# Two-layer streaming encoder in float32: the tail of the layer norms and the sums of the first one

## The chip, the cores and the metric

The kernel runs on one core of one Trainium2 chip. The metric is device microseconds of one execution. The kernel before takes 2613.07 us, the median of three runs (2607.23 to 2613.16). A core has a matrix engine (TensorE, PE in the profile, with its weight loads as PEld), a vector engine (VectorE, DVE), an engine for functions of one input (ScalarE, ACT), a general engine (GpSimd, POOL) and an engine that here issues most of the transfers (SyncE, SP). Each runs its own list of instructions in order, and they wait for one another by semaphores. Products accumulate in PSUM; everything else lies in SBUF.

## The reference, cut to what matters

One sequence of 1024 frames with 1024 channels passes through an RWKV-7 mixer, an MLP, a diagonal state-space mixer (S5) with a gated output, and a second MLP. After each of the four stands a layer norm of the residual sum:

```python
def layer_norm(x, g, b):
    xf = x.astype(jnp.float32)
    mu = jnp.mean(xf, axis=-1, keepdims=True)
    var = jnp.mean(jnp.square(xf - mu), axis=-1, keepdims=True)
    return ((xf - mu) * lax.rsqrt(var + LN_EPS) * g + b).astype(x.dtype)

x = layer_norm(DN_ALPHA * x + rwkv7_time_mix(x, ...), g0, b0)
x = layer_norm(DN_ALPHA * x + sq_relu_mlp(x, w1, w2), g1, b1)
x = layer_norm(DN_ALPHA * x + s5_mix(x, ...), g2, b2)
x = layer_norm(DN_ALPHA * x + sq_relu_mlp(x, w1, w2), g3, b3)
```

The last four lines are condensed; everything is float32.

## The kernel before, in words

Channels lie on the 128 partitions, frames along the free dimension. The 1024 frames are two halves of 512, called A and B below; a half of the activations is eight tiles of 128 channels by 512 frames (hA, hB).

A dense product is made of three TensorE products (L199). A weight tile `wraw` is loaded by SyncE, ScalarE rounds it to `whi` (L153) and VectorE makes the rest `wlo` = wraw − whi (L154). The input is split the same way into operand tiles (oAh and oAl for half A, oBh and oBl for B, qbuf in the MLPs). TensorE then adds hi·hi, hi·lo and lo·hi. There are two buffers for wraw and three each for whi and wlo, so a weight's next load waits for the split of an earlier one.

The recurrence of the first mixer is done in chunks, for each of which VectorE and ScalarE make the tables (KB, AR, PL, ldsg, elementwise work), TensorE makes matrices from them (pA), and a chain of small products steps the state: pR, pX, pU, pO (L716 to L737), each released by a copy `vsa` on ScalarE or VectorE. Half A's frames come first. After the fifth of its eight blocks the output product of half A and its layer norm are placed, and then half A's first MLP may begin while the recurrence of half B goes on.

Layer norm is called seven times by `layer_norm`, and the last half's last norm is a function of its own. The calls, in order of time: first norm, half A (at about 700 us) and half B (about 1180); second norm, A and B; third norm, A (about 1840) and B (about 1935); fourth norm, A. The first and the third make the operand tiles of the MLP behind them (`split_out`), the second and the fourth do not. A norm's steps are:

- mean: the eight tiles are added to one by GpSimd (two adds) and VectorE (five); a product with a matrix of ones, `pm`, sums over channels and spreads the mean over all partitions; VectorE subtracts it from the eight tiles (L883).
- variance: ScalarE squares each tile, VectorE and GpSimd add the squares to one tile (L891, L892), and four products of one column each, `pq` (L895), sum over channels with the frames on the partitions. VectorE adds epsilon (rs, L897), GpSimd takes the power −1/2, ScalarE spreads it (rb), and TensorE turns it into `pr`, the factor of each frame on all partitions.
- tail: VectorE multiplies each tile by pr (L906), ScalarE applies gain and offset in place (L907), and if operands are wanted `operand` splits the result: ScalarE rounds to the high part (L153), VectorE makes the low part (L154), except for tiles 1, 3 and 5 (`LNG`), whose low part GpSimd makes.

pm, pq and pr take turns in one PSUM bank (tag "l"). The squares have two buffers of each of two tags.

The order of each engine's instructions is not the order of the code. A scheduler places them by a rank: the code runs under `rank(...)`, lower numbers first, and a model of the engines' times decides among what is ready. The first norm, half A, has rank −1 (`LN1R`), ahead of all; the MLPs and the other norms come by their own ranks. The order is fixed when the kernel is built.

Of the kernel before, what the change touches and what calls it, by code (L numbers as in the profile page):

```python
# [8 lines left out]
F32 = mybir.dt.float32  # L9
F32R = mybir.dt.float32r  # L10
AF = mybir.ActivationFunctionType
# [8 lines left out]
KT = 8  # L20
# [7 lines left out]
LN1R = -1  # L28
WO0R = 99000
S5R = 300000  # L30
LNG = (1, 3, 5)
LNT = (2, 5)
TB = 2
JB = 4
# [39 lines left out]
def trunk(ctx, tc, A):  # L74
# [39 lines left out]
    def vec(n, k):  # L114
        i = PV.index(n)
        return pv[:, i, k : k + 1]
# [111 lines left out]
    def optile(H, hl):  # L228
        if H == 1:
            return sp.tile([128, HT], F32R, tag="oB" + hl, name="oB" + hl, bufs=8)  # L230
        return ap.tile([128, HT], F32R, tag="oA" + hl, name="oA" + hl, bufs=8)

    def operand(src, H=0, e=None):
        h, l = optile(H, "h"), optile(H, "l")
        split(src, h, l, e)
        return h, l
# [566 lines left out]
    def core():  # L803

        pg = rwkv_proj(0)
        next(pg)
        bulk.clear()
        with rank(3000):
            cur = elem(0)
        with rank(5000):  # L810
            amat(cur)
            invert(cur)
        with rank(100000):
            run(pg)
        last = None
        for m in range(8):
            if m == PB:
                with rank(100000):
                    run(rwkv_proj(1))
            if m == W0B:  # L820

                with rank(WO0R):
                    first_out.append(wo(0))
                with rank(LN1R):
                    first_out.append(layer_norm(first_out[0], 0, 0))
            base = m * 10000
            with rank(base + RK[0]):
                kbtrans(cur)
            nxt = None
            if m < 7:  # L830
                with rank(base + RK[1]):
                    nxt = elem(m + 1)
            if last and m in GB:
                with rank(base + RK[2]):
                    gnorm(last, 1)
            with rank(base):
                chain(cur, 0)
            if last and m not in GB:
                with rank(base + RK[2]):
                    gnorm(last, 1)  # L840
            if nxt and m < 6:
                with rank(base + RK[3]):
                    amat(nxt)
            with rank(base + RK[4]):
                chain(cur, 1)
            with rank(base + RK[5]):
                gnorm(cur, 0)
            if nxt:
                with rank(base + RK[6]):
                    if m == 6:  # L850
                        amat(nxt)
                    invert(nxt)
            last, cur = cur, nxt
        with rank(base + 8000):
            gnorm(last, 1)
# [4 lines left out]
            return ap.tile([128, HT + 1], F32, tag="xs", name="hA", bufs=8)[:, 0:HT]  # L860
        return sp.tile([128, HT], F32, tag="hB", name="hB", bufs=8)

    def layer_norm(h, gi, H, split_out=True):
        g, b = f"g{gi}", f"b{gi}"

        def lt(name, tag="la"):
            return tp.tile([128, HT], F32, tag=tag, name=name, bufs=2)

        def plt(name):
            return pl.tile([128, HT], F32, tag="l", name=name)  # L870

        a, b2 = lt("sa"), lt("sb")
        G.tensor_add(a, h[0], h[1])
        G.tensor_add(a, a, h[2])
        V.tensor_add(b2, h[3], h[4])
        for t in h[5:7]:
            V.tensor_add(b2, b2, t)
        V.tensor_add(b2, b2, h[7])
        V.tensor_add(a, a, b2)
        pm = plt("pm")  # L880
        PE.matmul(pm, ones_c, a, start=True, stop=True)
        for t in h:
            V.tensor_sub(t, t, pm)  # L883
        sa = [lt("sq0"), lt("sq1")]
        for k, t in enumerate(h):
            if k < 2:
                S.activation(sa[k], t, AF.Square)
            else:
                q = lt("sq", "m")
                S.activation(q, t, AF.Square)  # L890
                (G if k % 2 else V).tensor_add(sa[k % 2], sa[k % 2], q)  # L891
        V.tensor_add(sa[0], sa[0], sa[1])  # L892
        pq = plt("pq")
        for t in range(4):
            PE.matmul(pq[:, t : t + 1], sa[0][:, t * 128 : (t + 1) * 128], ones_c[:, 0:1], start=True, stop=True)  # L895
        rs = tp.tile([128, 4], F32, tag="rs", name="rs")
        V.tensor_scalar(rs, pq[:, 0:4], LN_EPS, None, op0=ALU.add)  # L897
        G.tensor_tensor(rs, rs, mhalf[:, 0:4], op=ALU.pow)
        rb = lt("rb").rearrange("p (t n) -> p t n", t=4)
        S.copy(rb, rs.unsqueeze(2).broadcast_to([128, 4, 128]))  # L900
        pr = plt("pr")
        for t in range(4):
            PE.transpose(pr[:, t * 128 : (t + 1) * 128], rb[:, t], ident)
        ops = []
        for k, t in enumerate(h):
            V.tensor_mul(t, t, pr)  # L906
            S.activation(t, t, AF.Identity, bias=vec(b, k), scale=vec(g, k))  # L907
            if split_out:
                ops.append(operand(t, H, G if k in LNG else V))
        return ops  # L910

    def last_norm(h, gi, c):
# [688 lines left out]
```

## Time and profile before

| | |
|---|---|
| median of three runs | 2613.07 us (2607.23 to 2613.16) |
| the profiled execution | 2617.01 us |
| its span in the trace | 2615.3 us |
| its mean granted TensorE clock | 0.971 |
| TensorE busy | 95% |
| VectorE, ScalarE, GpSimd busy | 69%, 47%, 17% |

In a row of the windows stand the start and end of a stretch, its length, then busy time and number of instructions of PE, PEld, DVE, ACT and POOL, the granted clock, the share of the DMA engines and the gigabytes per second. A row of the timeline has the start, the busy time of the instructions that it joins (their number behind x), the engine, the line, what is written and read, the shape, and in brackets the engine's idle time just before and what ended it. A row that begins with a line number sums up all instructions of a kind: number, shortest, median and longest duration in nanoseconds, first and last start.

### The profile page before, as it was taken

The page shows a single profiled execution, that of the slowest core. Times are in us where ns is not written, and L with a number is a line of the kernel's source. Part 1 is how long each engine was busy: PE and PEld are TensorE (multiplying, and loading weights), DVE is VectorE, ACT ScalarE, POOL GpSimd, SP SyncE. Part 2 cuts the span into 40 slices and gives each one's busy share as a digit, 9 for nine tenths or more (in the row PEclk, how much of TensorE's full clock was granted, in tenths as well). Part 3 has the DMA queues.
Part 4 walks back from the last instruction along what each step waited for, and adds up shares of the span by engine and source line. Part 5 has one row for each costly group of instructions (what it writes and reads, how often), then busy time and mean ns, then how long its engine had stood idle before and what let it go on. Part 6 is the DMA issues. An engine that isn't in the chain of part 4 may idle for free.

```text
span 2615.3 us, 43837 instructions
## 1 busy us (share of the span) xinstructions
PE 2473.6 (95%) x16624; PEld 2005.4 (77%) x16624; DVE 1813.5 (69%) x3459; ACT 1216.5 (47%) x2171; POOL 443.5 (17%) x372
## 2 busy tenths in 40 slices
PE   7999989999889999999999999999999999999997
PEld 5778767788667888776787888887777888888876
DVE  7366766787986766989886555777587555555576
ACT  7554575654454443345534333433464333433344
POOL 3121432332322001001000000201212111111011
PEclk9998979999989999999999999999999999999998
DMA  4765545554322324445465333253222111111133
GB/s 146 254 219 152 166 162 188 188 190 157 100 74 84 95 85 137 131 129 157 133 227 190 97 97 97 89 190 133 86 88 78 54 47 52 55 51 53 49 96 114
DMA packets 206291, 319.69 MB, mean 122 GB/s; under 512 B 20096, under 2 KB 80640, under 8 KB 206080
## 3 DMA queue, kind: packets, MB, share of 16 engines
q1 hardware_dynamic: 204928, 314.79, 38.2%
q8 instruction: 131, 2.15, 0.3%
q10 hardware_dynamic: 1152, 2.10, 0.2%
q14 instruction: 80, 0.66, 0.1%
HBM read 252.85 MB, written 63.96 MB: 121 GB/s over the span
## 4 chain that ended last, share of the span: by engine, by line
PE 61%; DVE 11%; DMA 3%; issue 2%; ACT 2%; POOL 1%; SPq 0%; ACTq 0%; DVEq 0%; POOLq 0%
PE d L199 46%; PE d L1048 9%; DVE wlo L154 2%; DMA wraw<-in_mw_dram 1%; DVE hA L1011 1%; DMA tt<-tT 1%; PE pA L608 0%; ACT whi L153 0%; PE py L1384 0%; PE pbu L1332 0%; PE pu L1320 0%; PE pk L1281 0%; DVE o L780 0%; DVE sq L891 0%; DVE xh L654 0%
## 5 line engine op out<-in xcount | busy, mean ns | idle before, releaser
L153 ACT CAST whi<-wraw 128x512 fp32r<-128x512 f32 x524 | 324.4, 620 | 680.3 <-PE d L199 465.0
L154 DVE TENSOR_TENSOR wlo<-wraw,whi 128x512 fp32r<-128x512 f32 x524 | 381.3, 728 | 260.2 <-ACT whi L153 255.2
L199 PE MATMUL d<-qbuf,whi 128*128 128x512 f32 (+1 forms) x1344 | 410.3, 389 | 12.8 <-DVE hA L1011 7.8
L199 PE MATMUL d<-oAh,whi 128*128 128x512 f32 (+1 forms) x768 | 308.9, 409 | 16.8 <-ACT ev L429 7.5
L199 PE MATMUL d<-oAh,wlo 128*128 128x512 f32 (+1 forms) x768 | 308.6, 406 | 10.2 <-DVE wlo L154 7.2
L199 PE MATMUL d<-oAl,whi 128*128 128x512 f32 (+1 forms) x768 | 308.0, 404 | 1.4 <-DVE oAl L154 1.4
L199 PEld LDWEIGHTS d<-qbuf,whi 128*128 128x128 f32 x1344 | 245.6, 190 | 67.6 <-DVE hA L1011 11.0
L199 PE MATMUL d<-qbuf,wlo 128*128 128x512 f32 (+1 forms) x672 | 257.2, 385 | 1.3 <-DVE wlo L154 1.1
L199 PE MATMUL d<-oBh,wlo 128*128 128x512 f32 x512 | 203.9, 399 | 3.4 <-DVE wlo L154 3.4
L199 PE MATMUL d<-oBh,whi 128*128 128x512 f32 x512 | 203.1, 397 | 2.4 <-ACT whi L153 2.0
L199 PE MATMUL d<-oBl,whi 128*128 128x512 f32 x512 | 201.4, 393 | 0.0
L199 PEld LDWEIGHTS d<-oAh,whi 128*128 128x128 f32 (+1 forms) x768 | 147.1, 193 | 53.9 <-ACT ev L429 9.7
L199 PEld LDWEIGHTS d<-oAh,wlo 128*128 128x128 f32 (+1 forms) x768 | 146.9, 192 | 46.0 <-DVE wlo L154 10.5
L199 PEld LDWEIGHTS d<-oAl,whi 128*128 128x128 f32 (+1 forms) x768 | 147.4, 193 | 33.3 <-DVE oAl L154 3.0
L199 PE MATMUL d<-qh,wlo 128*128 128x512 f32 x384 | 151.5, 395 | 0.0
L199 PE MATMUL d<-ql,whi 128*128 128x512 f32 x384 | 150.7, 392 | 0.0
L199 PE MATMUL d<-qh,whi 128*128 128x512 f32 x384 | 149.4, 389 | 0.0
L199 PEld LDWEIGHTS d<-qbuf,wlo 128*128 128x128 f32 x672 | 127.2, 190 | 27.9 <-DVE wlo L154 3.2
L1011 DVE TENSOR_TENSOR hB<-hB,d 128x512 f32<-128x512 f32 (+1 forms) x168 | 105.0, 633 | 33.2 <-PE d L199 31.4
L199 PEld LDWEIGHTS d<-oBh,wlo 128*128 128x128 f32 x512 | 96.8, 189 | 27.9 <-DVE wlo L154 4.8
L199 PEld LDWEIGHTS d<-oBh,whi 128*128 128x128 f32 x512 | 97.0, 189 | 24.0 <-ACT whi L153 2.6
L1011 DVE TENSOR_TENSOR hA<-hA,d 128x512 f32<-128x512 f32 x144 | 97.5, 682 | 24.2 <-PE d L199 23.1
(476 smaller groups left out, 5079.2 us busy)
## 6 DMA issues: line engine op xcount, KB each, us to landing
wraw<-in_mw_dram SPq DMA_DIRECT2D x376, 256.0 KB, 2.7
wraw<-in_glu_dram SPq DMA_DIRECT2D x64, 256.0 KB, 2.7
low<-wlo SPq DMA_DIRECT2D x52, 256.0 KB, 2.8
wlo<-low SPq DMA_DIRECT2D x52, 256.0 KB, 3.6
raw<-in_mw_dram SPq DMA_DIRECT2D x48, 256.0 KB, 2.6
wraw<-in_wk_dram SPq DMA_DIRECT2D x32, 256.0 KB, 3.8
wraw<-in_wr_dram SPq DMA_DIRECT2D x32, 256.0 KB, 3.6
wraw<-in_wv_dram SPq DMA_DIRECT2D x32, 256.0 KB, 4.5
```

The costliest lines, as they stand in the source:

```text
L153: S.copy(hi, src)
L154: (e or V).tensor_sub(lo, src, hi.bitcast(F32))
L199: bulk.append((PE.matmul(p, w, x, **kw).ins, x.shape[-1]))
L1011: V.tensor_add(z, z, p)
L1048: PE.matmul(p, w[:, k], x, start=not add and k + j == 0, stop=k == 3 and j == 2, skip_group_check=True)
```

## The change

All seven norms get another tail. VectorE multiplies deviation, gain and the frame's factor in one three-input operation. Where operands are wanted, ScalarE adds the offset and writes the rounded high part straight into the operand tile, and VectorE makes the low part, (t + b) − hi, in one three-input operation, for all eight tiles; GpSimd makes none. After that ScalarE adds the offset in place for the residual, tile by tile.

The first norm of half A alone (`by_pe`) also gets other sums. The mean's product takes three tiles in turn (the sum of tiles 0 to 2, the sum of 3 to 6, and tile 7) instead of their sum. The squares are not added by VectorE and GpSimd: each of the eight squared tiles goes through four products of one column that accumulate in pq, 32 instead of four.

```diff
-LNG = (1, 3, 5)
...
-                    first_out.append(layer_norm(first_out[0], 0, 0))
+                    first_out.append(layer_norm(first_out[0], 0, 0, True, True))
...
-    def layer_norm(h, gi, H, split_out=True):
+    def layer_norm(h, gi, H, split_out=True, by_pe=False):
...
-        V.tensor_add(b2, b2, h[7])
-        V.tensor_add(a, a, b2)
+        if by_pe:
+            parts = [a, b2, h[7]]
+        else:
+            V.tensor_add(b2, b2, h[7])
+            V.tensor_add(a, a, b2)
+            parts = [a]
         pm = plt("pm")
-        PE.matmul(pm, ones_c, a, start=True, stop=True)
+        for k, t in enumerate(parts):
+            PE.matmul(pm, ones_c, t, start=k == 0, stop=k == len(parts) - 1)
         for t in h:
             V.tensor_sub(t, t, pm)
...
+        pq = plt("pq")
+        if by_pe:
+            for k, t in enumerate(h):
+                q = lt("sq", ("la", "m")[k % 2])
                 S.activation(q, t, AF.Square)
-                (G if k % 2 else V).tensor_add(sa[k % 2], sa[k % 2], q)
-        V.tensor_add(sa[0], sa[0], sa[1])
...
+                for t4 in range(4):
+                    PE.matmul(pq[:, t4 : t4 + 1], q[:, t4 * 128 : (t4 + 1) * 128], ones_c[:, 0:1],
+                              start=k + t4 == 0, stop=k == KT - 1, skip_group_check=True)
+        else:
...
+                    (G if k % 2 else V).tensor_add(sa[k % 2], sa[k % 2], q)
+            V.tensor_add(sa[0], sa[0], sa[1])
...
         for k, t in enumerate(h):
-            V.tensor_mul(t, t, pr)
-            S.activation(t, t, AF.Identity, bias=vec(b, k), scale=vec(g, k))
+            V.scalar_tensor_tensor(t, t, vec(g, k), pr, op0=ALU.mult, op1=ALU.mult)
             if split_out:
-                ops.append(operand(t, H, G if k in LNG else V))
+                hi, lo = optile(H, "h"), optile(H, "l")
+                S.activation(hi, t, AF.Identity, bias=vec(b, k))
+                V.scalar_tensor_tensor(lo, t, vec(b, k), hi.bitcast(F32), op0=ALU.add, op1=ALU.subtract)
+                ops.append((hi, lo))
+        for k, t in enumerate(h):
+            S.activation(t, t, AF.Identity, bias=vec(b, k))
         return ops
```

The order of the instructions moves with it. Line numbers after the change are one less up to the norm and 16 more behind it. TensorE around the first norm, before (from the recurrence's pX to the norm's pq):

```order
L721 MATMUL pX<-o,XT 64x64 x8
L555 MATMUL pn<-ident,sq 128x128 x4
L726 MATMUL pU<-vsa,kbt 64x64 x8
L735 MATMUL pO<-st,AR 64x64 x8
L737 MATMUL pO<-vsa,AT_7145 64x64 x8
L584 MATMUL pb<-rksel,kf 64x1
L608 MATMUL pA<-AR,KB 128x128
L584 MATMUL pb<-rksel,kf 64x1 x15
L716 MATMUL pR<-vsa,AT_7145 64x64 x8
L608 MATMUL pA<-AR,KB 128x128 x7
L721 MATMUL pX<-o,XT 64x64 x8
L895 MATMUL pq<-ones_c,sq_7878 128x1 x4
```

And now:

```order
L885 MATMUL pm<-sa,ones_c 128x512
L885 MATMUL pm<-sb,ones_c 128x512
L885 MATMUL pm<-hA,ones_c 128x512
L715 MATMUL pR<-vsa,AT_7145 64x64 x2
L621 MATMUL pT<-ident,KB 128x128 x3
L554 MATMUL pn<-ident,sq 128x128 x4
L720 MATMUL pX<-o,XT 64x64 x8
L894 MATMUL pq<-ones_c,sq 128x1 x32
L725 MATMUL pU<-vsa,kbt 64x64 x8
L734 MATMUL pO<-st,AR 64x64 x8
L736 MATMUL pO<-vsa,AT_7145 64x64 x8
L583 MATMUL pb<-rksel,kf 64x1
```

The 32 pq products stand ahead of the recurrence's pU and pO; before, the four stood behind them, behind one more step's pR and pX and behind eight pA. In the whole program the recurrence's steps move back by about 100 dense products between here and the first norm of half B; from the S5 mixer of half B on only single products trade places.

VectorE in the same place, before:

```order
L891 TENSOR_TENSOR sq_7878<-sq_7878,sq 128x512
L713 COPY vsa<-st 64x256
L586 COPY bo<-pb 128x2x4
L780 SCALAR_TENSOR_TENSOR o<-o,vr,lg 128x64 x8
L558 SCALAR_TENSOR_TENSOR ldsg<-cmask,ldsg 128x512
L892 TENSOR_TENSOR sq_7878<-sq_7878,sq_7879 128x512
L562 COPY PL<-E 128x2x4
L612 TENSOR_TENSOR AT<-pA,amask 128x2x256
L572 TENSOR_TENSOR AR<-ldr,E 128x8x64
L612 TENSOR_TENSOR AT<-pA,amask 128x2x256
L722 COPY vsa<-pX 64x256
L897 TENSOR_SCALAR rs<-pq 128x4
```

And now:

```order
L763 TENSOR_SCALAR vr<-vr 128x8
L577 TENSOR_TENSOR KB<-lda,ldsg 64x8x64 x2
L557 SCALAR_TENSOR_TENSOR ldsg<-cmask,ldsg 128x512
L779 SCALAR_TENSOR_TENSOR o<-o,vr,lg 128x64 x8
L561 COPY PL<-E 128x2x4
L571 TENSOR_TENSOR AR<-ldr,E 128x8x64
L909 TENSOR_SCALAR rs<-pq 128x4
L728 TENSOR_TENSOR st<-pU,st 128x256
L729 TENSOR_TENSOR st<-st,PL 128x256
L712 COPY vsa<-st 64x256
L918 SCALAR_TENSOR_TENSOR hA<-hA,pv,pr 128x512 x8
L922 SCALAR_TENSOR_TENSOR oAl<-hA,pv,oAh 128x512 x4
```

The adds of the squares are gone; rs now stands ahead of the two AT operations, but still behind the table work (KB, the scan of ldsg, PL, AR) and the eight operations on o.

ScalarE at the third norm, half A, from its operands to the weight casts behind it, now (before, the affine results, the casts to oAh and the copies to t1r came in turn, tile by tile):

```order
L921 ACTIVATE oAh<-hA,pv 128x512 x4
L152 CAST whi<-wraw 128x512
L921 ACTIVATE oAh<-hA,pv 128x512 x4
L925 ACTIVATE hA<-hA,pv 128x512 x2
L1484 COPY t1r<-hA 128x512
L152 CAST whi<-wraw 128x512
L925 ACTIVATE hA<-hA,pv 128x512
L1484 COPY t1r<-hA 128x512
L1132 ACTIVATE sgl<-d 128x512
```

All high parts now come early, and the second whi stands seven operations behind the first; before, there were nine between these two.

More of the change, by code (lines that the diff above doesn't have):

```diff
@@ L877, in layer_norm @@
             V.tensor_add(b2, b2, t)
-        V.tensor_add(b2, b2, h[7])
-        V.tensor_add(a, a, b2)
+        if by_pe:
[4 more added lines that the diff above has]
+            parts = [a]
         pm = plt("pm")
-        PE.matmul(pm, ones_c, a, start=True, stop=True)
+        for k, t in enumerate(parts):
+            PE.matmul(pm, ones_c, t, start=k == 0, stop=k == len(parts) - 1)
         for t in h:
             V.tensor_sub(t, t, pm)
[L884 to L889, printed above, removed]
-                S.activation(q, t, AF.Square)
[L891 to L895, printed above, removed]
+        pq = plt("pq")
+        if by_pe:
+            for k, t in enumerate(h):
+                q = lt("sq", ("la", "m")[k % 2])
+                S.activation(q, t, AF.Square)
+                for t4 in range(4):
+                    PE.matmul(pq[:, t4 : t4 + 1], q[:, t4 * 128 : (t4 + 1) * 128], ones_c[:, 0:1],
+                              start=k + t4 == 0, stop=k == KT - 1, skip_group_check=True)
+        else:
+            sa = [lt("sq0"), lt("sq1")]
+            for k, t in enumerate(h):
+                if k < 2:
+                    S.activation(sa[k], t, AF.Square)
+                else:
+                    q = lt("sq", "m")
+                    S.activation(q, t, AF.Square)
+                    (G if k % 2 else V).tensor_add(sa[k % 2], sa[k % 2], q)
+            V.tensor_add(sa[0], sa[0], sa[1])
+            for t in range(4):
+                PE.matmul(pq[:, t : t + 1], sa[0][:, t * 128 : (t + 1) * 128], ones_c[:, 0:1], start=True, stop=True)
         rs = tp.tile([128, 4], F32, tag="rs", name="rs")
@@ L905, in layer_norm @@
         for k, t in enumerate(h):
-            V.tensor_mul(t, t, pr)
-            S.activation(t, t, AF.Identity, bias=vec(b, k), scale=vec(g, k))
+            V.scalar_tensor_tensor(t, t, vec(g, k), pr, op0=ALU.mult, op1=ALU.mult)
             if split_out:
-                ops.append(operand(t, H, G if k in LNG else V))
+                hi, lo = optile(H, "h"), optile(H, "l")
+                S.activation(hi, t, AF.Identity, bias=vec(b, k))
+                V.scalar_tensor_tensor(lo, t, vec(b, k), hi.bitcast(F32), op0=ALU.add, op1=ALU.subtract)
+                ops.append((hi, lo))
+        for k, t in enumerate(h):
+            S.activation(t, t, AF.Identity, bias=vec(b, k))
         return ops
```

## The prediction, made before the change was timed

> **What bounds the kernel now.** I read the page's busy shares and its chain of waits first, then the windows around each norm, then the timelines of TensorE (PE), VectorE (DVE) and the others there.
>
> ```profile
> span 2615.3 us, 43837 instructions
> PE 2473.6 (95%) x16624; PEld 2005.4 (77%) x16624; DVE 1813.5 (69%) x3459; ACT 1216.5 (47%) x2171; POOL 443.5 (17%) x372
> PE 61%; DVE 11%; DMA 3%; issue 2%; ACT 2%; POOL 1%; SPq 0%; ACTq 0%; DVEq 0%; POOLq 0%
> ```
>
> TensorE is busy 95% of the span and is 61% of the chain that ended last. Work taken off another engine therefore counts only where TensorE stands idle or runs at a lower clock. The windows (PE, PEld, DVE, ACT, POOL busy us; then the granted clock) show where that is:
>
> ```profile
> 700.00:720.00 20.00, 10.19 (x136) 8.87 (x136) 19.75 (x30) 7.52 (x15) 15.51 (x11) 0.73 0.21 62
> 720.00:740.00 20.00, 18.71 (x146) 14.71 (x147) 17.56 (x33) 12.35 (x22) 5.15 (x4) 0.76 0.08 27
> 740.00:760.00 20.00, 17.27 (x126) 13.09 (x127) 16.49 (x50) 11.62 (x22) 6.89 (x5) 0.91 0.31 91
> 1540.00:1560.00 20.00, 20.00 (x89) 16.48 (x88) 10.92 (x17) 8.31 (x14) 0.00 (x0) 1.00 0.32 98
> ```
>
> The last row is the ordinary state: 89 dense products in 20 us, 0.225 us each, no idle time. The first three are the first norm (first half, after the recurrence's output product). In 700–720 TensorE is idle half of the time at clock 0.73, while VectorE is full. This stretch is where the change does most.
>
> ```profile
> 702.76 1.12 PE L726 MATMUL pU<-vsa,kbt 128*64 128x64 f32 x16 [4.60 <-ACT vsa L723]
> 712.55 1.60 PE L716 MATMUL pR<-vsa,AT 128*64 128x64 f32 x16 [4.93 <-ACT vsa L712]
> 718.69 1.12 PE L895 MATMUL pq<-ones_c,sq 128*128 128x1 f32 x8 [1.92 <-DVE sq L892]
> 728.61 1.50 PE L608 MATMUL pA<-AR,KB 64*128 64x128 f32 x14
> 730.04 0.73 PE L199 MATMUL d<-oAh,whi 128*128 128x512 f32 x2
> 744.99 0.50 PE L199 MATMUL d<-oAh,whi 128*128 128x512 f32 x1 [1.67 <-ACT whi L153]
> 746.78 0.77 PE L199 MATMUL d<-oAh,whi 128*128 128x512 f32 x1 [1.06 <-ACT whi L153]
> 750.30 0.39 PE L199 MATMUL d<-oAh,wlo 128*128 128x512 f32 x1
> 753.35 0.69 PE L726 MATMUL pU<-vsa,kbt 128*64 128x64 f32 x16
> ```
>
> Dense products on the norm's output begin at 730.04 and run without waits from 750.3. The same pU group takes 1.12 us at 702.76 and 0.69 at 753.35, after the idle stretch and away from it.
>
> **The first norm, part by part.** Here the squares' sum and a part of the mean's sum go to TensorE.
>
> ```profile
> 695.08 1.10 PE L881 MATMUL pm<-sa,ones_c 128*128 128x512 f32 x2 [0.41 <-DVE rn L549]
> 696.22 4.87 DVE L883 TENSOR_TENSOR hA<-hA,pm 128x512 f32<-128x512 f32 x8 [1.13 <-PE pm L881]
> 708.11 3.49 DVE L578 TENSOR_TENSOR KB<-lda,ldsg 64x512 f32<-64x512 f32 x2
> 711.63 0.37 SPq L525 DMA_DIRECT2D ldsg<-s_sg  x1
> 713.22 2.67 DVE L780 SCALAR_TENSOR_TENSOR o<-o,vr,lg 128x64 f32<-128x64 f32 x8
> 722.07 0.16 DVE L897 TENSOR_SCALAR rs<-pq 128x4 f32<-128x4 f32 x1
> 725.84 4.87 DVE L906 TENSOR_TENSOR hA<-hA,pr 128x512 f32<-128x512 f32 x8 [1.21 <-PE pr L903]
> 737.83 1.88 DVE L154 TENSOR_TENSOR oAl<-hA,oAh 128x512 fp32r<-128x512 f32 x3
> L891 POOL TENSOR_TENSOR sq<-sq,sq x21: 1259/1305/1773, 700.5 to 2524.1; 128x512 f32<-128x512 f32 x21
> ```
>
> TensorE gains work. One pm product is one row of two passes, 1.10 us, whose starts lie 0.51 apart; two more are about 2.04 us. pq was one group, 1.05 to 1.12 us; eight groups are 7 × 1.05 = 7.35 us more. That is 9.4 us, and the idle time in 700–720 alone is 9.8. I count it as filling.
>
> VectorE loses two adds for the mean, three for the squares and the last one: 6 × 0.61 to 0.68 (eight subtractions take 4.87), about 4 us; GpSimd (POOL) loses three adds of 1.305.
>
> Now when the operands come. pm ends about 0.8 us later (two more products, two VectorE adds less ahead of it), the subtractions end at 702. pq shares pm's PSUM bank, so it starts after them; with the last squares its products end at about 710.4, against 719.8 before. But rs stands in VectorE's order behind both KB operations (3.49 us), a scan that needs the load issued at 711.63, eight operations of L780 (2.67 us), PL and AR. Those keep their times, so rs goes from 722.07 to about 717.2: of the 9.4 us gained on pq, half is lost in that queue. The multiplies start 3.8 us behind rs as before, at about 721.
>
> ```profile
> L906 DVE TENSOR_TENSOR hA<-hA,pr x32: 679/680/689, 725.8 to 2544.1; 128x512 f32<-128x512 f32 x32
> L648 DVE SCALAR_TENSOR_TENSOR xh<-xa,emask,xh x8: 748/756/756, 174.4 to 899.9; 128x512 f32<-128x512 f32 x8
> L1404 DVE SCALAR_TENSOR_TENSOR yg<-hB,pv,pyt x8: 1149/1165/1292, 1739.8 to 1801.5; 128x512 f32<-128x512 f32 x8
> L907 ACT ACTIVATE hA<-hA,pv x32: 800/806/818, 726.6 to 2547.7; 128x512 f32<-128x512 f32 x32
> L349 ACT ACTIVATE ev<-ev,half x32: 704/718/747, 53.7 to 358.8; 128x512 f32<-128x512 f32 x32
> L153 ACT CAST oAh<-m x40: 600/618/626, 8.5 to 558.4; 128x512 fp32r<-128x512 f32 x40
> ```
>
> The new multiply is a three-input operation with a per-partition factor. No row has it with a plain PSUM operand and this order. Its bounds are 0.68 (nothing added, L906) and 1.165 (L1404, which reads with a stride); L648, also 512 columns without a stride, is nearest, so I take 0.75. It prices the new low-part operation too: eight of them instead of five at 0.68, so VectorE gets 8 × 0.07 + 8 × 0.75 − 5 × 0.69 = 3.1 us more at each norm that makes operands. ScalarE had 0.81 + 0.61 for each tile; now it has 0.72 (high part) and 0.72 (residual, after all high parts): the same sum, but the last high part no longer stands behind the affine results. The last low part is then at 721 + 8 × 0.68 + 8 × 0.75 = 732.4, against 739.7: 7.3 us earlier.
>
> Not all of it reaches TensorE, which by then has more of the recurrence to do: the order shifts those steps about 100 dense products later. By my walk, at 734 it still lacks, against the state of before at 750.3, 21 dense products (21 × 0.225 = 4.7), some 31 pA (1.50 for 14, so 0.09 to 0.1 each, 2.9) and six groups like pU (6 × 0.69 = 4.1): 11.7 us, which ends at 745.7. With no wait in it the gain is 4.6. Before, that stretch lost 1.67 + 1.06 on weight casts and some 1.6 to the lower clock (from 746.78 to 750.30 eight products start, 0.44 apart instead of 0.23), 4.3 in all; if the casts, now queued behind eight residual operations, lose as much, 0.3 is left. Between 0.3 and 4.6 I take the middle: **−2.5 us**.
>
> The later place of the recurrence's steps and tables costs nothing while TensorE is full, as in 1540–1560: each step takes as long in any place. If a table comes too late for its reader, one wait like those at 702.76 or 712.55 follows, up to +5; I take 0.
>
> **The other three norms with operands.** Their sums stay as they were; the tail changes. Two of them have TensorE waits of their own:
>
> ```profile
> 1847.60 0.61 ACT L153 CAST whi<-wraw 128x512 fp32r<-128x512 f32 x1
> 1848.26 0.50 PE L199 MATMUL d<-oBh,whi 128*128 128x512 f32 x1 [2.03 <-ACT whi L153]
> 1849.39 3.43 DVE L154 TENSOR_TENSOR wlo<-wraw,whi 128x512 fp32r<-128x512 f32 x2
> 1850.56 3.41 POOL L154 TENSOR_TENSOR oAl<-hA,oAh 128x512 fp32r<-128x512 f32 x2
> 1851.20 0.80 PE L199 MATMUL d<-oBh,wlo 128*128 128x512 f32 x1 [2.20 <-DVE wlo L154]
> 1853.07 0.63 PE L199 MATMUL d<-oBh,whi 128*128 128x512 f32 x1
> 1942.44 1.76 DVE L154 TENSOR_TENSOR wlo<-wraw,whi 128x512 fp32r<-128x512 f32 x1
> 1944.26 0.50 PE L199 MATMUL d<-oAh,wlo 128*128 128x512 f32 x1 [2.27 <-DVE wlo L154]
> L154 DVE TENSOR_TENSOR wlo<-wraw,whi x524: 649/690/1791, 43.5 to 2593.2; 128x512 fp32r<-128x512 f32 x175
> ```
>
> A weight's low part takes 0.69 us at the median, but 1.7 while GpSimd makes a norm's low part; GpSimd's three of each norm now go to VectorE. Some ten VectorE operations are stretched so, about 1 us each, three at a norm, so VectorE's 3.1 us more is about paid back. At 1848 the cast that TensorE waits for stands seven ScalarE operations behind the weight cast before it in the new order, not nine, and the low part of 1849.39 ends, by adding up the operations ahead of it from the norm's multiplies on, at 1849.3 instead of 1851.1: −1.9. At 1944 the low part stands behind six operations instead of seven and isn't stretched: about −1.4. I take **−3.3** for both together; 0 if the waits only pass to weight loads, and −10 if they vanish (2.03 + 2.20 + 2.27, and 3.5 for some 18 products that start 0.43 apart, as from 1851.20 to 1853.07). The fourth (second half, around 1180) lies where VectorE is full for long and neutral by the sum above: 0. The three norms without operands save 8 × 0.09 us of ScalarE each, beside a full TensorE: nothing.
>
> The page "SBUF — State Buffer" of the Trainium skill (Who interferes with whom) says that a VectorE operation with two SBUF inputs and a GpSimd operation that reads SBUF exclude one another for a whole instruction, while one with a PSUM input does not take part. The rows at 1849.39 and 1850.56 agree. Taken strictly it would free every stretched operation, which is the second case below.
>
> **Sum.** −2.5 − 3.3 = −5.8 on the profiled execution's 2617.01 us: 2611.2. That execution lies 3.9 us above the median of the runs, 2613.07, so on their scale 2607.3, say **2607**. A change under 0.3%, 7.8 us, can't be told from none here: faster is below 2605.2, slower above 2620.9.
>
> **The rivals.**
> - Forecast, chance 0.44: 2607, own range 2600 to 2614; of it 0.17 lies below 2605.2.
> - All three places run without waits, 0.24: −4.6 − 10 = −14.6, 2598. For it: each wait named there ends on a cast or a low part that moves forward. Against: the loads of weights follow the low parts that free their buffers, and may wait next.
> - The operands come early to no use, 0.16: the casts behind eight residual operations, and the weight loads, keep TensorE's waits as long as they were. About 2613, within the 0.3%.
> - Slower, 0.12: the 32 pq products stand ahead of pU in TensorE's fixed order, so the recurrence's next step waits for the last square. If dense products can't yet fill (they need operands that come at about 722 at the earliest), the 9.4 us of added work pushes the chain of recurrence steps instead of filling: 2613 + 9.4 = 2622. It decides if pU then starts 7 us or more later than at 702.76 and TensorE is still not full at 750.
> - The three-input operation costs 1.165 instead of 0.75, 0.04: 16 × 0.415 = 6.6 us at each norm with operands; three of them lie where VectorE is what TensorE waits for, and half is hidden: +10 on the forecast, 2617 to 2622, slower when nothing is gained elsewhere.
>
> Faster: 0.17 + 0.24 = 0.41. Same: 0.27 + 0.16 = 0.43. Slower: 0.16. The range is 2597 to 2621.
>
> **What would show it.** The changed profile should have the last of 32 pq products near 710, rs near 717, the last low part of the first norm near 732 and dense products without waits from about 747; GpSimd with no low part of a norm; weights' low parts of 0.69 us at 1850 and 1943, with waits there of about 1 us less each; the new operations at 0.75 (VectorE) and 0.72 (ScalarE). It is wrong if rs isn't earlier (the queue, not pq, sets it), if the weights' waits around 1850 and 1944 are as long or longer, or if TensorE's time from 2000 on, where the order is nearly unchanged, shifts at all.

## The result and the profile after

The changed kernel takes 2619.30 us (median of 16 runs, 2610.60 to 2632.91). The kernel before, run beside it, takes 2613.11 (16 runs, 2603.31 to 2622.60). The ratio is 1.0030 with a 95% interval of 1.0015 to 1.0044: slower by 0.3%, some 8 us. Forecast was 2607, faster by 6.

The page of the changed kernel's profiled execution (2621.09 us), span, busy shares and chain that ended last:

```profile
span 2619.4 us, 43946 instructions
PE 2482.9 (95%) x16684; PEld 2012.7 (77%) x16684; DVE 1808.2 (69%) x3465; ACT 1216.0 (46%) x2171; POOL 424.0 (16%) x357
PE 58%; DVE 8%; DMA 2%; ACT 2%; issue 2%; SPq 0%; POOL 0%; ACTq 0%; DVEq 0%; POOLq 0%
```

VectorE and GpSimd have less to do (1808 instead of 1814 us, 424 instead of 444), TensorE 9.3 us more, and the span is 4.1 us longer. The first norm, TensorE's timeline:

```profile
642.80 0.69 PE L725 MATMUL pU<-vsa,kbt 128*64 128x64 f32 x16
...
687.71 1.12 PE L885 MATMUL pm<-sa,ones_c 128*128 128x512 f32 x2
688.67 1.02 PE L885 MATMUL pm<-sb,ones_c 128*128 128x512 f32 x2
689.53 1.02 PE L885 MATMUL pm<-hA,ones_c 128*128 128x512 f32 x2
...
695.61 13.03 PE L894 MATMUL pq<-ones_c,sq 128*128 128x1 f32 x64 [3.27 <-DVE hA L887]
708.57 1.13 PE L725 MATMUL pU<-vsa,kbt 128*64 128x64 f32 x16
...
718.88 1.22 PE L198 MATMUL d<-oAh,whi 128*128 128x512 f32 x2
```

And VectorE's:

```profile
707.74 1.23 DVE L557 TENSOR_TENSOR_SCAN ldsg<-cmask,ldsg 128x512 f32<-128x512 f32 x1 [4.82 <-DMA ldsg<-s_sg]
711.22 0.16 DVE L909 TENSOR_SCALAR rs<-pq 128x4 f32<-128x4 f32 x1
715.33 5.36 DVE L918 SCALAR_TENSOR_TENSOR hA<-hA,pv,pr 128x512 f32<-128x512 f32 x8 [2.41 <-PE pr L915]
726.25 1.42 DVE L922 SCALAR_TENSOR_TENSOR oAl<-hA,pv,oAh 128x512 fp32r<-128x512 f32 x2
```

This execution was 6.3 us ahead of the one of before already at the recurrence's pU of 649 (642.80 here), before the changed work, so absolute times mislead. From the first pm product on: pq ends at +20.9 (before: 695.08 to 719.81, +24.7), rs starts at +23.5 (+27.0), the last low part ends at +40.0 (+44.6). The operands come 4.6 us earlier. But the 32 pq products are one block of 13.03 us, and pU stands behind it: 65.8 us after its group at 642.80, where it was 53.7 (649.10 to 702.76), so 12 us later. The chain makes this delay up within two steps: the second pU group behind this one starts at 746.43, 103.6 us after the group at 642.80, and its counterpart before at 753.35, 104.3 us after.

In the windows of the changed kernel the clock is at 0.50 through that stretch, and VectorE is full in 1100 to 1150; the last row is the kernel before:

```profile
700.00:720.00 20.00, 17.92 (x145) 16.14 (x145) 12.66 (x26) 8.40 (x16) 7.16 (x6) 0.50 0.17 52
720.00:740.00 20.00, 19.75 (x165) 15.76 (x164) 16.76 (x32) 13.06 (x25) 4.72 (x4) 0.91 0.25 80
1100.00:1150.00 50.00, 45.80 (x199) 36.09 (x200) 49.12 (x91) 20.03 (x36) 2.54 (x2) 0.90 0.25 80
```

```profile
1100.00:1150.00 50.00, 49.58 (x240) 39.11 (x238) 46.32 (x81) 21.21 (x39) 2.92 (x2) 1.00 0.31 97
```

Before, TensorE was 99% busy there at full clock; now it is 92% busy at 0.90. The lead is lost at such places. One of them, changed kernel, VectorE and TensorE:

```profile
1131.14 1.22 DVE L1261 TENSOR_TENSOR b<-bc,q 128x1024 f32<-128x1024 f32 x1
1132.27 4.86 DVE L887 TENSOR_TENSOR hB<-hB,pm 128x512 f32<-128x512 f32 x8
1137.06 0.68 DVE L1027 TENSOR_TENSOR hA<-hA,d 128x512 f32<-128x512 f32 x1
```

```profile
1137.79 1.22 PE L198 MATMUL d<-qbuf,whi 128*128 128x512 f32 x2 [3.36 <-DVE hA L1027]
```

TensorE waits 3.36 us until VectorE has emptied a product's PSUM tile (hA at 1137.06), which stands behind the eight subtractions of half B's first norm and, ahead of them, work on the S5 tables (L1261 is the last of it).

To compare kernels, I take the stretch from the pU group at 649 to the second norm's mean product of half B at 1666. Everything that the first norm moves lies in it, and from 1430 on TensorE is full.

```profile
649.10 0.69 PE L726 MATMUL pU<-vsa,kbt 128*64 128x64 f32 x16
...
1666.12 1.02 PE L881 MATMUL pm<-sa,ones_c 128*128 128x512 f32 x2
```

That is 1017.0 us before; the changed kernel has 1022.9 (642.80 to 1665.68), 5.9 longer.

### The profile page after: what moved, and what is told of

The parts are those of the page before. It is cut to its first block, busy times and chain, and to the rows that moved or that the text cites. A ratio compares the mean times of both kernels' runs of the same rounds, so it can differ in the third digit from the quotient of the medians.

```text
span 2619.4 us, 43946 instructions
## 1 busy us (share of the span) xinstructions
PE 2482.9 (95%) x16684; PEld 2012.7 (77%) x16684; DVE 1808.2 (69%) x3465; ACT 1216.0 (46%) x2171; POOL 424.0 (16%) x357
## 4 chain that ended last, share of the span: by engine, by line
PE 58%; DVE 8%; DMA 2%; ACT 2%; issue 2%; SPq 0%; POOL 0%; ACTq 0%; DVEq 0%; POOLq 0%
PE d L198 44%; PE d L1064 9%; DVE wlo L153 1%; DMA wraw<-in_mw_dram 1%; DVE hA L918 1%; PE pk L1297 1%; ACT whi L152 0%; DMA yl<-s_y 0%; PE pu L1336 0%; PE pA L607 0%; DVE qbuf L153 0%; DVE hB L918 0%; PE pyt L1418 0%; PE py L1408 0%; DVE oBl L922 0%
## 5 line engine op out<-in xcount | busy, mean ns | idle before, releaser
L198 PE MATMUL d<-qbuf,whi 128*128 128x512 f32 (+1 forms) x1344 | 415.9, 392 | 20.1 <-DVE hA L1027 7.1
```

The source lines that it names most:

```text
L198: bulk.append((PE.matmul(p, w, x, **kw).ins, x.shape[-1]))
```

## The experiments

Ratios are to the kernel before, run beside each variant. "Stretch" is the change of the stretch of 1017.0 us in the one profiled execution. Two executions with the same order of instructions there differed by up to 3.5 us (the changed kernel and e4, which differ only behind it: 5.9 and 9.4), so a single value is worth no more than that. "Block 6" with a number says how many dense products stand ahead of the recurrence's block 6 in TensorE's order: 2361 in the kernel before, 2469 in the changed one.

### e1, e2, e3, e4: the parts alone

Theory A: the first norm gains, VectorE's full stretch takes it back, and the loss is made at the third norm of half B. Its waits in the changed kernel were longer than the 0.73, 2.27 and 1.30 of before:

```profile
1942.32 0.50 PE L198 MATMUL d<-oAh,wlo 128*128 128x512 f32 x1 [1.55 <-DVE wlo L153]
1946.95 1.21 PE L198 MATMUL d<-qbuf,whi 128*128 128x512 f32 x4 [1.62 <-ACT whi L152]
1954.07 1.22 PE L198 MATMUL d<-qbuf,whi 128*128 128x512 f32 x2 [3.61 <-ACT rl L1010]
```

Theory B: the added TensorE work is the loss.

e1, the sums alone:

```diff
-            V.scalar_tensor_tensor(t, t, vec(g, k), pr, op0=ALU.mult, op1=ALU.mult)
...
+            V.tensor_mul(t, t, pr)
+            S.activation(t, t, AF.Identity, bias=vec(b, k), scale=vec(g, k))
+            if split_out:
+                ops.append(operand(t, H, G if k in LNG else V))
```

> The first norm's sums on TensorE alone; all seven tails as before (LNG kept). Theory A (the place decides): the first norm ends earlier, as in the changed kernel, but VectorE's full stretch from about 1050 to 1430 gives the lead back, and the added 9.4 us of TensorE work is paid there; the loss of the changed kernel lies at the third norm, which is as before here. So 2608 to 2616 (ratio 0.998 to 1.001). Theory B (the added TensorE products are the loss): TensorE is 95% busy, so 9.4 us more work costs nearly all of it, 2619 to 2623 (1.0025 to 1.004).

Measured 1.0013 (0.9996 to 1.0031), stretch +4.3, block 6 at 2463: between the two theories, a loss of about 3 us that the timing alone can't tell from none.

e2, the tails alone:

```diff
-                    first_out.append(layer_norm(first_out[0], 0, 0, True, True))
+                    first_out.append(layer_norm(first_out[0], 0, 0))
```

> The new tail at all seven norms; the first norm's sums as before (by_pe off). Theory A: the third norm of half B loses TensorE time as in the changed kernel (waits of 1.55, 1.62 and 3.61 us around 1940 to 1954, against 0.73, 2.27 and 1.30 before), some 4 us, less about 2 at the third norm of half A: 2615 to 2621 (1.001 to 1.003). Theory B: no added TensorE products, and operands earlier: 2606 to 2612 (0.997 to 0.9995).

Measured 0.9989 (0.9976 to 1.0002), stretch −2.1, block 6 at 2399. Theory A wanted a loss. So it is the sums, not the tails, that move the recurrence past 2460. The same kernel was run again:

> The kernel of e2 once more, to narrow its interval (0.9976 to 1.0002): new tails at all seven norms, first norm's sums as before. If the tail is a gain of 2 to 3 us, 0.998 to 0.9995 again; if it is nothing, 0.9995 to 1.001.

Measured 0.9951 (0.9932 to 0.9970), stretch −2.8. The two intervals don't meet, so the size is uncertain by more than the intervals say, but beside the old sums the tails are a gain.

e3, both parts at the first norm, the other six tails as in e1:

> The whole change at the first norm alone (its sums and its tail); the other six norms as before. Theory A: the lead of the first norm, some 11 us in TensorE's progress at 850 in the changed kernel, is still there at 850 and gone by 1430, and nothing is lost later: 2609 to 2615 (0.9985 to 1.0005). Theory B: 2618 to 2623, as in the changed kernel, since the added work is all here.

Measured 1.0020 (1.0005 to 1.0036), stretch +2.3: the loss is made with the first norm changed alone.

e4, the changed kernel with the tail of e1 at the third norm of half B only:

> The changed kernel with the old tail at one norm, the third of half B (about 1935). Theory A: the wait of 3.61 us there goes back to about 1.3 and the time to 2613 to 2616 (ratio to before 1.000 to 1.001, 4 us under the changed kernel). Theory B: this norm's tail is neutral, 2618 to 2621 (1.002 to 1.003).

Measured 1.0025 (1.0013 to 1.0036), stretch +9.4. Undoing the place where theory A put the loss leaves the time as it was. Theory A falls as to where the loss is made.

### e5, e13: pq done twice

From here on theory W says that added TensorE work is paid wherever it stands, and theory O that the loss is the later place of the recurrence in TensorE's order.

e5, each product twice, the second into columns that nobody reads:

```diff
                 for t4 in range(4):
-                    PE.matmul(pq[:, t4 : t4 + 1], ...)
+                    for u in range(2):
+                        PE.matmul(pq[:, 4 * u + t4 : 4 * u + t4 + 1], ...)
```

> The changed kernel with each of the 32 pq products done twice (the second result is written to columns that nobody reads); the order is otherwise the same. In the changed kernel's trace the 32 products take 13.0 us (695.6 to 708.6) at a clock of 0.50. Theory W (the added TensorE work is paid, since TensorE bounds the whole): 8 to 13 us more than the changed kernel, 2627 to 2632, ratio to before 1.006 to 1.008. Theory O (the later place of the recurrence in TensorE's order is the loss; it is not moved further here): the added work falls ahead of dense products that only come later by as much, and the lead that is lost anyway shrinks: 2618 to 2622, ratio 1.002 to 1.004.

Measured 1.0072 (1.0057 to 1.0088), stretch +20.7: as theory W had it. TensorE and VectorE there:

```profile
696.35 26.38 PE L895 MATMUL pq<-ones_c,sq 128*128 128x1 f32 x128 [3.27 <-DVE hA L887]
```

```profile
722.76 0.16 DVE L910 TENSOR_SCALAR rs<-pq 128x4 f32<-128x4 f32 x1 [12.83 <-PE pq L895]
```

The block doubles to 26.4 us, and the loss grows by 11. But rs now waits 12.83 us for pq: the doubling delays the norm itself, not only what stands behind. The same with pq behind pU (e8 below), where theory O puts the loss on pq's place ahead of pU, and W on the work:

> The kernel of e8 (pq behind pU) with every pq product done twice (second result unused); TensorE's order is that of e8. Theory O (the loss is that pq stands ahead of the recurrence's pU, not its work): behind pU the doubled work falls into idle time or delays only the next step, and most of it is hidden: 0 to 5 us over e8, 2612 to 2619, ratio to before 1.000 to 1.0025; e5, with the same work ahead of pU, was 1.0072. Theory W (the work is paid wherever it stands): 8 to 13 us over e8, 2622 to 2628, ratio 1.0035 to 1.0055.

Measured 1.0038 (1.0023 to 1.0052), stretch +14.7: 9 us over e8, as theory W had it. Here too rs waits for the block, so neither run tells work from delay. What they show is that most of 13 us more is not hidden in this stretch.

### e8, e9, e10: the place in TensorE's order

e8, pq behind pU by one order edge:

```diff
+            if m == W0B:
+                tc.add_manual_dep(late[0].ins, hops[-1][2], ...)   # first pq, last pU
```

> The changed kernel with one order edge more: the first pq product stands behind the last product of the recurrence's pU, instead of ahead of it. The recurrence's next block then stands 56 dense products earlier than in the changed kernel and 52 later than before. Theory W: same work, so as the changed kernel, 2617 to 2621 (1.002 to 1.0035). Theory O: pU comes 10 us earlier than in the changed kernel, half of the delay is gone: 2612 to 2616 (1.000 to 1.0015).

Measured 1.0004 (0.9992 to 1.0015), stretch +2.8: as theory O had it, 7 us better than the changed kernel with the same work.

```profile
707.61 1.12 PE L725 MATMUL pU<-vsa,kbt 128*64 128x64 f32 x16
708.66 13.81 PE L897 MATMUL pq<-ones_c,sq 128*128 128x1 f32 x64
725.65 1.11 PE L918 MATMUL pr<-ident,rb 128*128 128x128 f32 x4
```

pU is 3.5 us late instead of 12 (57.2 us after its group at 650.44), but the block then delays what stands behind it, and the operands are only 1.8 us earlier than before (last low part +42.8). The edge also put the recurrence's block 6 at 2413 dense products instead of 2469 (2361 before), so two things changed at once. e9 moves only the place, in the kernel before:

```diff
+    tc.add_manual_dep(hops[6][0], bulk[nb + 316][0].name, ...)   # block 6 behind dense product 316 of the MLP
```

> The kernel before with one order edge: the first product of the recurrence's block 6 stands behind dense product 316 of the first MLP, so that this block and the next stand where the changed kernel has them (about 110 dense products later than before). No work is added, the norms are as before. Theory W: 2610 to 2614 (0.999 to 1.001). Theory O: the S5 tables and the second half's output product follow later, and the time rises as in the changed kernel: 2616 to 2622 (1.0015 to 1.004).

Measured 1.0018 (1.0007 to 1.0030), stretch +7.2. With no work added and no norm changed, the later place of blocks 6 and 7 costs some 5 us, as theory O had it (what the scheduler places around them moves along).

e10 forces the early place in the changed kernel:

```diff
+    for k in range(229, 429):
+        tc.add_manual_dep(bulk[nb + k][0], hops[6][2].name, ...)
```

> The changed kernel with order edges: 200 dense products of the first MLP, from the 229th on, stand behind block 6's first pU, so that the recurrence's blocks 6 and 7 stand where the kernel before has them (2362 dense products ahead of it, 2469 in the changed kernel, 2361 before). Theory W: the work stays, 2617 to 2621 (1.002 to 1.0035). Theory O: 2609 to 2614 (0.9985 to 1.001). If TensorE waits for block 6 there, up to 5 us on top for both.

Measured 1.0040 (1.0026 to 1.0055), stretch +5.8: no cure, and theory O's number missed. But TensorE now stands still for block 6:

```profile
818.59 1.92 PE L665 MATMUL pv<-x,AT 32*32 32x32 f32 x64 [5.96 <-DVE x L658]
```

Block 6's inverse (x) isn't ready that early, and with the waits of the steps behind it TensorE is idle for 9.4 us between 812 and 830, where neither the changed kernel nor the kernel before waits at all. So e10 speaks neither for nor against the place.

### e11, e12: versions that beat both

e11 is e2 with the old tail at the third norm of half B:

> The kernel of e2 (new tails, first norm's sums as before) with the old tail at the third norm of half B. Over the traces so far the third norm of half A is 4 us shorter with the new tail (six traces with it, four without), that of half B 2 us longer (five with, five without). If that holds: 2 us under e2, 2603 to 2610, ratio to before 0.997 to 0.9992. If the tail is neutral at B, as the timing of e4 against the changed kernel had it: as e2, 0.998 to 1.000.

Measured 0.9974 (0.9960 to 0.9989), stretch −5.0. Beside e2_again's 0.9951, measured together with it, this shows no gain from the old tail there.

e12 is e11 with pq of the first norm summed from the two tiles of squares that VectorE and GpSimd make, without their last add:

```diff
-            V.tensor_add(sa[0], sa[0], sa[1])
-            for t in range(4):
-                PE.matmul(pq[:, t : t + 1], sa[0][:, t * 128 : (t + 1) * 128], ...)
+            for k in range(2):
+                for t in range(4):
+                    PE.matmul(pq[:, t : t + 1], sa[k][:, t * 128 : (t + 1) * 128], ...)
```

> The kernel of e11, and at the first norm pq is summed from the two tiles of squares (8 products instead of 4), so that the last add on VectorE goes away (1.69 us in the trace of before, just ahead of pq). Theory O: this takes an operation off the queue that rs waits in and adds 1 us of TensorE work behind pU: 0 to 2 us under e11, ratio 0.996 to 0.999. Theory W: 1 us more than e11 at most, 0.9975 to 0.9995.

Measured 0.9977 (0.9962 to 0.9991), stretch −7.0; again, later:

> The kernel of e12 once more, beside the others of this job: 0.996 to 0.999 again, 2603 to 2611. Not below 0.999 would mean that its gain is not settled.

0.9974 (0.9960 to 0.9989), stretch −5.7, median 2605.53. TensorE and VectorE of e12:

```profile
692.79 1.91 PE L887 MATMUL pm<-sa,ones_c 128*128 128x512 f32 x2
...
711.59 1.87 PE L910 MATMUL pq<-ones_c,sq 128*128 128x1 f32 x8
716.01 1.86 PE L910 MATMUL pq<-ones_c,sq 128*128 128x1 f32 x8
```

```profile
717.91 0.16 DVE L917 TENSOR_SCALAR rs<-pq 128x4 f32<-128x4 f32 x1
...
732.48 0.74 DVE L937 SCALAR_TENSOR_TENSOR oAl<-hA,pv,oAh 128x512 fp32r<-128x512 f32 x1
```

The last low part ends 40.4 us after pm's start: the whole lead of the changed kernel (40.0) with 8 pq products instead of 32. It beats both kernels, though not e11 by anything that can be told.

### e14, e15, e16: work and place apart

e14 splits pq's block: 8 products ahead of pU, 12 behind it, 12 behind the next pR:

```diff
+                for k, step in ((8, 2), (20, 3)):
+                    tc.add_manual_dep(late[k].ins, hops[-1][step], ...)   # behind pU; behind the next pR
```

> The changed kernel with two order edges: of the 32 pq products 8 stand ahead of the recurrence's pU, 12 between this pU and the next step's pR, 12 between that and pX; all the work is kept. Blocks 6 and 7 stand as late as in the changed kernel (2463 dense products ahead of block 6). If the added work is paid wherever it stands: as the changed kernel, 1.002 to 1.004. If the block ahead of a step is the loss, what stays is the later place alone: 1.000 to 1.002. If both the block and the place cost nothing more: under 1.000.

Measured 1.0029 (1.0013 to 1.0046), stretch +4.4: as the changed kernel, and as the first of the three expectations had it.

```profile
702.20 2.91 PE L898 MATMUL pq<-ones_c,sq 128*128 128x1 f32 x16 [3.26 <-DVE hA L891]
707.00 1.12 PE L725 MATMUL pU<-vsa,kbt 128*64 128x64 f32 x16
708.06 5.28 PE L898 MATMUL pq<-ones_c,sq 128*128 128x1 f32 x24
```

pU is some 4 us late instead of 12 (57.6 us after its group at 649.4), and the operands are as early as in the changed kernel (+40.4). Neither shows in the time while blocks 6 and 7 stand late (2463). e16 puts them at 2403 by edges like those of e10:

> The kernel of e14, with blocks 6 and 7 put where the tail-only kernels have them (2403 dense products ahead of block 6; 2399 there). If the added work is paid wherever it stands: 1.002 to 1.004. If block and place are the loss: 0.997 to 0.9995, as the tail-only kernels. A wait of TensorE for block 6, as in e10, would add up to 5 us and show as such.

Measured 1.0013 (0.9997 to 1.0029), stretch −2.7 in a profiled execution (2603.96 us) that was the fastest of this kernel, whose median is 2616.21. Between the two theories; 4 us better than e14. The waits that were expected to show are there: between 807 and 816 TensorE stands idle for 4.2 us at block 6 (0.20 to 1.38 us each, for results of ScalarE), and the granted clock is 0.83 from 800 to 820. The trace of e12, with block 6 at 2399, has no wait there.

e15 gives e12 the late place (2486 instead of 2399), by the edge of e9:

> The kernel of e12 with blocks 6 and 7 as late as in the changed kernel (2486 dense products ahead of block 6 instead of 2399), by one order edge; no work is added. If the later place costs as in e9: 3 to 7 us over e12, 0.9985 to 1.001. If e9 was a fluke: as e12, 0.996 to 0.999.

Measured 1.0009 (0.9994 to 1.0023), stretch +7.3, against 0.9974 and −5.7 of the same kernel without the edge, measured together with it: 9 us for the place alone.

## Why the prediction was wrong

Read by times, three terms add up to about the result. Each is a mean of three, and uncertain by about 0.1%:

| term | from | per mille | us |
|---|---|---|---|
| new tails | e2, e2_again, e11 (0.9989, 0.9951, 0.9974) | −2.9 | −7.5 |
| 32 pq products, as against few, at like place | e16 − e12, e8 − e12, e14 − e15 (+3.8, +2.8, +2.0) | +2.9 | +7.5 |
| blocks 6 and 7 later | e9, e15 − e12_again, e14 − e16 (+1.8, +3.5, +1.6) | +2.3 | +6 |
| sum | | +2.3 | +6 |
| measured | | +3.0 (1.5 to 4.4) | +8 |

That they add up doesn't show the split. The pairs of the second row also differ in the mean's products, and e8, e14 and e16 in the tail of one later norm. e16 carries the 4.2 us of waits for block 6 (1.6 per mille), which the table books as products, and takes off the place. And one pair is missing: e1 and e9 both have the old tails and a late block 6 (2463, 2486), and e1, with the 32 products, is 0.5 per mille the faster. By the table e1 would be at 1.0052; it was measured at 1.0013 (0.9996 to 1.0031). With e16 put right and this pair counted, I estimate +1.6 for the products and +2.8 for the place. From e1 to the changed kernel, moreover, the tails are no gain (1.0013 to 1.0030). What is shown is the place (e9, and e15 beside e12_again, with no work added) and the gain of the tails beside the old sums; the price of the products is not settled.

**The prices of single operations were right.** The new multiply takes 0.743 (0.75 forecast), the high part 0.71 and the residual 0.72 (0.72 forecast), the low part 0.744 where GpSimd isn't beside it:

```profile
L918 DVE SCALAR_TENSOR_TENSOR hA<-hA,pv,pr x32: 734/743/748, 715.3 to 2548.6; 128x512 f32<-128x512 f32 x32
L921 ACT ACTIVATE oAh<-hA,pv x16: 707/710/724, 716.1 to 1843.7; 128x512 fp32r<-128x512 f32 x16
L922 DVE SCALAR_TENSOR_TENSOR oAl<-hA,pv,oAh x16: 736/744/1773, 720.6 to 1847.9; 128x512 fp32r<-128x512 f32 x16
L925 ACT ACTIVATE hA<-hA,pv x32: 709/722/731, 722.3 to 2551.6; 128x512 f32<-128x512 f32 x32
```

The rival with 1.165 for the three-input operation is out.

**pq was mis-sized.** I took 1.05 us a group from a row of eight passes, 8.4 us in all. It takes 13.03. The passes start 0.11 apart at first and 0.21 once the clock is at 0.50. So pq ends 3.8 us earlier after pm than before, not 9.4, and the last low part 4.6 earlier, not 7.3. That rs waits in VectorE's queue was right in kind: its scan waited 4.82 us for the ldsg load, and rs started 2.6 us after pq's end.

**"I count it as filling" failed in part.** The idle time of 700 to 720 was waits of the recurrence's steps and of the norm on one another. A product put there stands ahead of one of them: of pU in the changed kernel (12 us late; 5.8 us later than 702.76 on the clock of its execution, which was 6.3 us ahead), of pr and the next step in e8. The slower rival (chance 0.12) named this, with pU late by 7 us or more and 2622 as its time; 2619.30 was measured. Its other condition, TensorE not yet full at 750, didn't hold: it waits little from 718.88 on, and 720 to 740 has 19.75 of 20 busy. The delay isn't what cost the time either: the chain had made it up two steps later, and e14, with pU 4 us late, took as long as the changed kernel. That 2619 lies near this rival's 2622 is luck. Where blocks 6 and 7 stand early, the products do cost (e8 beside e12, +2.8 per mille); where they stand late, the signs disagree (e14 − e15 +2.0 and e1 − e9 −0.5 per mille; the stretches of e1, e3, e14, the changed kernel and e4 are +2.3 to +9.4, those of e9 and e15, without the products, +7.2 and +7.3).

**The recurrence's later place, put at 0, is the failed term that the runs show best.** My ground was that TensorE is full there, so a step costs the same in any place. That holds for the step; it overlooked what is behind the recurrence. e9 and e15 show +5 and +9 us for the place alone. The traces show where. Take as lost, of the time from one TensorE instruction's start to the next, what goes beyond the 20th percentile for its kind in the kernel before. In all eight kernels with block 6 behind 2460 or more dense products (the changed one, e1, e3, e4, e5, e9, e14, e15) the lost time between 850 and 1450 is 9.5 to 15.6 us more than in the kernel before; in the nine other traces, with it at 2413 or earlier, it is 0.2 more to 5.5 less. That is not the net price, since the late kernels lose less at first: by the same measure e9 loses some 6 us less than the kernel before in the 200 us behind its pU group and some 13 more after that, which makes its +7.2. The changed kernel loses some 16 less in those 200 us, for some 9 us of added work priced alike, and some 14 more after that. So up to there the idle time did take the products in, and the lead was lost later, as in e9. The dense products done early are a lead only on paper; as I read it, the postponed steps, S5 tables and half B's norm then crowd on VectorE. That VectorE's queue is the carrier rests on rows like those at 1132 to 1137 alone; no run took that queue away, so it is argued and not shown.

**The third norms.** For half A the forecast was −1.9, and more was found. From its mean product to that of half B's third norm, the 14 traces with the new tail there are 2.1 to 5.2 us shorter than before (mean 3.9), the other three with the old tail 0.1 shorter to 1.6 longer. TensorE's waits there in the changed kernel are 0.52 to 1.75, where 2.03 and 2.20 stood:

```profile
1849.89 0.50 PE L198 MATMUL d<-oBh,wlo 128*128 128x512 f32 x1 [0.82 <-DVE wlo L153]
1853.46 0.50 PE L198 MATMUL d<-oBh,wlo 128*128 128x512 f32 x1 [0.54 <-DVE wlo L153]
1858.24 0.50 PE L198 MATMUL d<-oBh,whi 128*128 128x512 f32 x1 [1.75 <-ACT whi L152]
```

For half B the forecast was −1.4 and the step failed: I moved the low part of one weight forward but didn't follow what comes behind. Changed kernel, VectorE and then ScalarE:

```profile
1942.19 4.44 DVE L922 SCALAR_TENSOR_TENSOR oBl<-hB,pv,oBh 128x512 fp32r<-128x512 f32 x5
1946.56 0.68 DVE L1503 TENSOR_TENSOR t1r<-t1r,hB 128x512 f32<-128x512 f32 x1
1947.16 0.68 DVE L153 TENSOR_TENSOR wlo<-wraw,whi 128x512 fp32r<-128x512 f32 x1
```

```profile
1952.38 0.62 ACT L152 CAST whi<-wraw 128x512 fp32r<-128x512 f32 x1 [3.12 <-DMA wraw<-in_mw_dram]
```

The next weight's low part stands behind five low parts of the norm, the load into its buffer follows that, the cast waits 3.12 us for the load, and `rl`, behind the cast on ScalarE, is what TensorE waits 3.61 us for. From this norm's mean product to that of the fourth norm, the nine traces with the new tail there are 2.0 to 4.3 us longer than before (mean 2.8), the other eight, with the old tail, 0.0 to 2.8 (mean 1.3): where a gain of 1.4 was forecast, the new tail is some 1.5 us behind the old, though the two groups overlap. Against that e4 and e11, with the old tail there, were not faster than their partners; what this place costs in time stays open.

The tails' total, −7.5, is larger than the −3.3 that I gave the third norms; alone they come out at about 2606 on the scale of 2613, where I had put the whole change. That is near the forecast by luck: half A's third norm gave more and half B's less than I said. The rival in which the operands come early to no use fits the first norm: e12 has them 3.5 us earlier than e11 (+40.4, +43.9) and the same time.

Three things stay open. No run shows why the products cost where the recurrence stands early and don't clearly cost where it stands late. Whether 13 us of products that delay no step would be free wasn't tried: in every variant they stood ahead of something. And the three terms are from medians whose runs scatter by 10 us; the two runs of e2 differ by more than their intervals.

## What to carry to other kernels

Before you count idle time of the busiest engine as free, look up which instruction follows the gap in that engine's order, and give the added block its whole length as that one's delay; here that was 12 of 13 us. Then follow the chain further, since it may make the delay up, as it did here. Above all, compare the whole order: the added work moved other work. When a scheduler moves a chain back "because the engine is full anyway", price what hangs on the end of that chain on the other engines. And take a saving at its knee: dropping the last add on VectorE brought the operands as early with 8 products as 32 products did, though neither lead showed in the time.

## What the runs showed of the hardware that I had not expected

Products of one column didn't bring the clock back. In the changed kernel TensorE is idle for 3.27 us ahead of 695.61, then busy without a gap to 708.6 with 64 passes of 128x1. The granted clock falls 0.8 us into the block, which may still be due to the idle time, and stays down:

```profile
690.00:695.00 5.00, 2.34 (x29) 1.49 (x27) 4.41 (x8) 3.56 (x7) 0.31 (x1) 1.00 0.19 52
695.00:700.00 5.00, 4.39 (x25) 4.42 (x25) 4.89 (x8) 1.62 (x3) 3.03 (x3) 0.64 0.12 34
700.00:705.00 5.00, 5.00 (x25) 5.00 (x25) 2.90 (x3) 2.05 (x4) 4.34 (x4) 0.50 0.21 68
```

In the third row TensorE is busy all of the time, with 25 passes 0.21 us apart and as many weight loads, at a clock of 0.50. In e5 the clock stays at 0.50 from the 12th pass to the end of the 26.38 us. The dense products that begin at 718.88 in the changed kernel have it at 1.00 from 724 on, after 5 us. The page "TensorE: Matmul & The Clock Gate" of the Trainium skill (Part 1) says that the clock is gated by how busy the array has been of late; the trace agrees only if a pass of one column hardly counts as busy, since TensorE is busy all the time in the profile while the clock stays at half. What the clock does count, no run here shows.

Low parts made by VectorE with a per-partition offset still take up to 1.77 us beside GpSimd's work (the maximum of the L922 row, at 721.26, while GpSimd makes kf from 720.68 to 722.48; the median is 0.744). So moving GpSimd's share to VectorE doesn't free the two of one another as long as GpSimd has other operations there.
